# A macaron block on one core: two block-product chunks instead of one in the last down product

## The chip, the core and the metric

The kernel runs on one NeuronCore of a Trainium2 chip. The metric is the device time of one execution in microseconds; the median of the runs counts. Engines go by the profile's names: PE is TensorE (PEld its weight load), DVE VectorE, ACT ScalarE, POOL GpSimd, SP SyncE. SBUF is the memory on the core that all engines work from, PSUM the eight banks into which PE accumulates.

## What is computed

One layer: a feed-forward network at half weight, a mixer of short convolution and gated linear attention, a second feed-forward network at half weight, and a last norm. Sequence 512, model width 1024, hidden width 2816, all in float32. What matters here is the second feed-forward network and the norm behind it:

```python
def rmsnorm(x, g):
    xf = x.astype(jnp.float32)
    y = xf * lax.rsqrt(jnp.mean(xf * xf, axis=-1, keepdims=True) + EPS)
    return (y * g.astype(jnp.float32)).astype(x.dtype)

def swiglu(x, w_gu, w_down):
    g, u = jnp.split(x @ w_gu, 2, axis=-1)
    return (jax.nn.silu(g) * u) @ w_down
...
x = x + FFN_RES_WEIGHT * swiglu(rmsnorm(x, norm_ffn2_g[l]), ffn2_w_gu[l], ffn2_w_down[l])
return rmsnorm(x, final_norm_g)
```

The change is in the last product, `(...) @ w_down` of the second network: 512 x 2816 times 2816 x 1024, that is 22 k tiles of 128.

## The kernel before

**Precision.** Each float32 operand is split into a high half, a cast on ACT, and a low half, a subtraction on DVE; a product is three matmuls (high x high, high x low, low x high).

**Weights.** All weights lie in one array in the order of `PLAN`, in units of 128 x 1024 or less. `STEPS` lists the order in which units are used. The class `Weights` loads units into the pool `f` (10 buffers of 128 x 1024), by DMAs that SP issues, and splits them into `wh` and `wl` (3 buffers each) two units ahead of the one that PE takes (`take`, `issue`). The last four tiles split into `op` instead.

**Block products.** Most of the matrix products are done in the seven-product form of a 2 x 2 block product: seven block products instead of eight, at the price of sums of blocks before and after. The products are called m1, p2, q6, p5, q7, p3, p4. Weight blocks are a11, a12, a21, a22. m1 uses a11, p2 a12, p4 a22. DVE makes s3 = a11 + a21 in another f buffer (line 320), which q7 uses. POOL issues accumulating DMAs (line 310) that add one f buffer to another in place: a22 into a21 (then p5 uses a21), a21 into a11 once m1 is done with it (then q6 uses a11), a11 into a12 once p2 is done with it (then p3 uses a12). The class `Operands` makes the seven operands of the other side; p5, q6, q7 and p4 need a sum on DVE first (lines 556 to 563), made in place, and each is split into two `op` buffers of 128 x 1024 (lines 576 and 577; 14 buffers).

**The last product.** `last_down` works in three stages. First, ten plain k tiles (8 to 17), each 24 matmuls of 512 columns (4 blocks of the sequence, 2 halves of the output, 3 matmuls; lines 778 to 780) into all eight PSUM banks; their operands are split by `split_hid`, two tiles at a time (lines 691 and 692). After them eight adds on DVE carry the banks into the residual `X` (line 787). In between, the operands of the chunk are made, in the order of the list `more`. Then the chunk, k tiles 0 to 7, by seven block products. Each product is taken in two units, which use two weight buffers of 2 k tiles each, and each unit is 12 matmuls of 512 columns into a pair of banks (line 829). After each product two adds of 128 x 512 on DVE carry its pair into `X`. Bank pair b serves m1, q6, q7 and p4, pair a serves p2, pair c serves p5 and p3; six banks are in the pool `ps`, two more in `pa`. Last, four plain tiles (18 to 21, `TAIL`), taken bank by bank, with the last norm and the stores behind each.

**Order.** The order on PE is the order of the code. The queues of the other engines are ordered when the kernel is built: of what is ready and finds a buffer, the instruction that stands first in the code goes first. So loads and splits run ahead as far as their buffers allow. `loads`, `sums` and `pre` in `Weights.phase` say at which step of `STEPS` a chunk's loads, its s3 sums and the tail's loads stand in the code.

Of the kernel before, what the change touches and what calls it, by code (L numbers as in the profile page):

```python
# [15 lines left out]
P = 128  # L16
# [4 lines left out]
KF = DFF // P  # L21
# [19 lines left out]
TAIL = 4  # L41
# [23 lines left out]
def full(mat, kt):  # L65
    return [(mat, k, 1, (0,), 1024) for k in range(kt)]
# [12 lines left out]
HW = 256  # L79
# [24 lines left out]
PLAN = []  # L104
STEPS = []
# [3 lines left out]
def units(us):  # L109
    for u in us:  # L110
        STEPS.append((len(PLAN), None))
        PLAN.append(u)
# [17 lines left out]
CHUNK = 8  # L130
CHUNK_ORDER = ("m1", "p2", "q6", "p5", "q7", "p3", "p4")
CHUNK_STEP = {}


def last_plan(down):
    us = full(down, KF)
    units(us[CHUNK : KF - TAIL])
    firsts = []
    for s in range(2):
        firsts.append(len(PLAN))  # L140
        PLAN.extend((down, 4 * j + 2 * s, 2, (512 * i,), 512) for i in range(2) for j in range(2))
    CHUNK_STEP.update({(s, p): len(STEPS) + 2 * i + s for i, p in enumerate(CHUNK_ORDER)
                       for s in range(2)})
    STEPS.extend((n, p) for p in CHUNK_ORDER for n in firsts)
    units(us[KF - TAIL :])


def ffn_plan(up, down, plain, slow):

    units(group(up, KD, (0, DFF, P, DFF + P), slow))  # L150
    for f in range(2, plain):
        units(single(up, KD, f * P))
        units(single(up, KD, DFF + f * P))
    sets(up, [(s * HW, DFF + s * HW) for s in range(plain // 2, KF // 2)])
    if slow:
        us = full(down, KF)
        units(us[CHUNK : KF - TAIL1])
        sets(down, [(2 * s * HW, (2 * s + 1) * HW) for s in range(D // (2 * HW))])
        units(us[KF - TAIL1 :])
    else:  # L160
        last_plan(down)
    ENDS.append(len(STEPS))
# [33 lines left out]
def block_kernel(ctx: ExitStack, tc: tile.TileContext, xT, vecs, gf, gup, wgl, wts, out):  # L196
    nc = tc.nc
# [12 lines left out]
    def phase(odd, **bufs):  # L210

        stack = ExitStack()
        for n, b in bufs.items():
            pools[n] = stack.enter_context(
                tc.tile_pool(name=n if n != "small" else odd, bufs=b, reuse_waits="tile"))
        return stack

    def tile_of(pool, shape, dtype=F32):
        cnt[0] += 1
        return pools[pool].tile(shape, dtype, tag=pool, name=f"{pool}{cnt[0]}")  # L220
# [4 lines left out]
    def MM():  # L225
        cnt[0] += 1
        return ps.tile([P, S], F32, tag="mm", name=f"mm{cnt[0]}")

    def AUX():
        cnt[0] += 1  # L230
        return pa.tile([P, S], F32, tag="aux", name=f"aux{cnt[0]}")
# [23 lines left out]
    class Weights:  # L255
# [14 lines left out]
        def phase(self, early, first=6):  # L270


            self.early = early
            lo, self.end = self.end, [e for e in ENDS if e > self.end][0]
            for i in range(lo, self.end):
                n, p = STEPS[i]
                if p == "m1" and i in CHUNK_STEP.values():
                    at = CHUNK_STEP[0, "m1"]
                    self.loads.setdefault(at - (4 if i == at else 2), []).append(n)
                    self.sums.setdefault(i, []).append(n)  # L280
                elif p is None and i > lo and STEPS[i - 1][1] is not None and self.end < len(STEPS):
                    self.pre.setdefault(i - 4, []).append(n)
                elif p == "m1":
                    self.loads.setdefault(max(lo, i - first), []).append(n)
                    first = 6
                    self.sums.setdefault(max(lo + 3, i - 3), []).append(n)
            if self.end == len(STEPS):
                c = CHUNK_STEP
                for i, at in enumerate((c[1, "q6"], c[1, "p3"], c[1, "p3"], c[1, "p4"])):
                    self.pre.setdefault(at, []).append(STEPS[self.end - TAIL + i][0])  # L290
            self.fetch(lo)

# [244 lines left out]
    class Operands:  # L537
# [29 lines left out]
        def make(self, p):  # L567
            if p in self.parts:
                return
            i = self.ORDER.index(p)  # L570
            if i > 0:
                self.make(self.ORDER[i - 1])
            v = self.sum(p)
            h, l = (tile_of("op", [P, 1024], F32R) for _ in range(2))
            hv, lv = (t.rearrange("p (k t) -> p k t", t=HW) for t in (h, l))
            nc.scalar.copy(hv, v)  # L576
            nc.vector.tensor_tensor(out=lv, in0=v, in1=hv.bitcast(F32), op=ALU.subtract)  # L577
            self.parts[p] = (h, l)
# [23 lines left out]
    def ffn(up, down, norm, nxt, plain, at):  # L602
# [93 lines left out]
        if nxt is None:  # L696
            return last_down(us, hid, split_hid)
# [67 lines left out]
    def last_down(us, hid, split_hid):  # L765
# [7 lines left out]
        o = [[MM(), MM()] for t in range(NTB - 1)] + [[AUX(), AUX()]]  # L773

        def mm(t, e, k, w, hl):
            wh, wl = (a[:, 512 * e : 512 * (e + 1)] for a in w)
            a, b = (v[:, k % 2, t * P : (t + 1) * P] for v in hl)
            nc.tensor.matmul(o[t][e], a, wh, start=k in (CHUNK, KF - TAIL), stop=False)  # L778
            nc.tensor.matmul(o[t][e], a, wl, start=False, stop=False)  # L779
            nc.tensor.matmul(o[t][e], b, wh, start=False, stop=k in (KF - TAIL - 1, KF - 1))  # L780

        def blocks(t):
            return t.rearrange("p (d i) -> p d i", i=P)
# [1 line left out]
        def add(t, e, bank, by):  # L785
            xt = X[:, 4 * e : 4 * e + 4, t * P : (t + 1) * P]
            nc.vector.scalar_tensor_tensor(out=xt, in0=blocks(bank), scalar=by, in1=xt,
                                           op0=ALU.mult, op1=ALU.add)

        ho = Operands(lambda j, l: hid[:, 4 * j : 4 * j + 4, l * HW : (l + 1) * HW])  # L790
        hls = {k: split_hid(k) for k in (CHUNK, CHUNK + 2)}
        more = [4, 6, 8, "m1", "p2", "p5", "q6", "q7", "p3"]
        for k in range(CHUNK, KF - TAIL):
            w = W.take(us[k])
            for t in range(NTB):
                for e in range(2):
                    mm(t, e, k, w, hls[k - k % 2])
            if more:
                n = more.pop(0)
                if isinstance(n, int):  # L800
                    hls[CHUNK + n] = split_hid(CHUNK + n)
                else:
                    ho.make(n)
        for t in range(NTB):
            for e in range(2):
                add(t, e, o[t][e], 0.5)
        ho.make("p4")


        uses = {"m1": [(0, 0, 0.5)], "p2": [(0, 0, 0.5)], "q6": [(1, 0, 0.5)],  # L810
                "p5": [(1, 1, -0.5)], "q7": [(1, 1, -0.5)], "p3": [(1, 0, 0.5)],
                "p4": [(0, 1, -0.5)]}
        banks = {}
        for p in CHUNK_ORDER:
            b = {"p2": "a", "p5": "c", "p3": "c"}.get(p, "b")
            fresh = b not in banks
            if fresh:
                banks[b] = [MM(), MM()]
            bh, bl = ho.get(p)
            for s in range(2):  # L820
                h, l = W.take()
                for i in range(2):
                    k = 2 * s + i
                    wh, wl = (a[:, 512 * i : 512 * (i + 1)] for a in (h, l))
                    for e in range(2):
                        c = slice(k * HW + e * P, k * HW + (e + 1) * P)
                        to = banks[b][e]
                        for n, (aa, ww) in enumerate(((bh, wh), (bh, wl), (bl, wh))):
                            nc.tensor.matmul(to, aa[:, c], ww,  # L829
                                             start=fresh and k == 0 and n == 0,  # L830
                                             stop=k == 3 and n == 2, skip_group_check=True)
            for l, e, by in uses[p]:
                for t in range(2):
                    add(2 * l + t, e, banks[b][t], by)
        o[:] = [[MM(), MM()] for t in range(NTB - 1)] + [[AUX(), AUX()]]
        w = [W.take(u) for u in us[KF - TAIL :]]
        hl = [split_hid(k) for k in range(KF - TAIL, KF, 2)]
# [41 lines left out]
        with tc.manual_schedule(engines={ENG.PE, ENG.DVE, ENG.Activation}):  # L879
# [4 lines left out]
            for t in range(NTB):  # L884
                sm = front.tile([P, 8], F32, tag="fin", name=f"fin{t}", bufs=2)
                f = [sm[:, i : i + 1] for i in range(6)]
# [502 lines left out]
    with phase("small1", **FFN):  # L1389
        W.phase(1)  # L1390
        n1 = Norm(V_G1)
        for k in range(KD):
            nc.sync.dma_start(x[k], xT[k])
            if k < 2 or k == 3:
                W.issue()
        W.early = 5
        for k in range(KD):
            n1.add(k, sooner=True)
        nm = Norm(V_GM)
        ffn("ffn1_w_gu", "ffn1_w_down", n1, nm, PLAIN1, 5)  # L1400
    with phase("small2", f=10, tp=6, v=4, qk=2, g=1, y=4, small=1):
        W.phase(4, 5)
        n2 = Norm(V_G2)
        mixer(nm, n2)
    with phase("small3", **FFN):
        W.phase(5)
        ffn("ffn2_w_gu", "ffn2_w_down", n2, None, PLAIN2, 5)
# [43 lines left out]
```

## Time and profile before

| | |
|---|---|
| median of 3 runs | 1197.54 us (1197.14 to 1198.35) |
| span of the profiled execution | 1196.1 us |
| its median less its span | 1.4 us |
| PE busy | 1188.1 us, 99% |
| DVE busy | 830.7 us, 69% |
| ACT busy | 587.3 us, 49% |
| ten plain tiles of the last product | 54.42 us, from 1074.95 |
| the chunk | 38.08 us, from 1129.37 |
| the four tail tiles | 21.78 us, from 1167.45 |

The profile gives no time of its own for the profiled execution beside its span; the span runs from the first to the last instruction of the program, and the runs' times contain what lies around it. In the rows of the profile, L829 is line 829 of the kernel before, `out<-in` are the names of the tiles written and read, and what stands in brackets is how long the engine was idle before the instruction and what ended that. `<-` names the releaser, which is inferred. A matmul's duration includes its pipeline, so matmuls overlap, and a stage's length over their count is their pace.

### The profile page before, as it was taken

To read this page: it belongs to the slowest core of one execution; us is meant where nothing else is said; L and a number is where in the kernel's file an instruction comes from. 1 tells how busy PE (TensorE), PEld (TensorE's weight loads), DVE (VectorE), ACT (ScalarE), POOL (GpSimd) and SP (SyncE) were. 2 spreads that over 40 slices of the span, in tenths; PEclk is the share of its full clock that TensorE was granted. 3 is DMA by queue.
4 is the path that set the end of the run, shared out by engine and by line. 5 is a ranking of instruction groups with operands and counts; after the bars stand their busy time and mean duration, and the time that the engine had idled before them with its cause. 6 is when DMAs were issued, how large, how long until landed. Compare 5 with 4: busy or idle time off the path is not lost.

```text
span 1196.1 us, 19145 instructions
## 1 busy us (share of the span) xinstructions
PE 1188.1 (99%) x7858; PEld 1095.6 (92%) x7858; DVE 830.7 (69%) x997; ACT 587.3 (49%) x730; POOL 101.2 (8%) x137
## 2 busy tenths in 40 slices
PE   9999999999999999999999999999999999999997
PEld 8899999988988889999999998888889999998886
DVE  7976566844787765858678686555597656675685
ACT  6564444622354465646454574324355455562353
POOL 0011111000110001011011100100001111100100
PEclk9999999999999999999999999999999999999999
DMA  9377777533473225767767766613338777763431
GB/s 346 87 207 187 180 184 187 176 101 80 104 270 106 88 66 146 201 183 188 191 179 175 190 185 211 203 48 141 120 74 209 167 188 173 186 180 108 93 95 70
DMA packets 57607, 187.65 MB, mean 157 GB/s; under 512 B 6480, under 2 KB 10704, under 8 KB 57520
## 3 DMA queue, kind: packets, MB, share of 16 engines
q1 hardware_dynamic: 36912, 124.27, 29.5%
q0 software_dynamic: 15968, 57.68, 26.1%
q10 hardware_dynamic: 4640, 4.49, 1.2%
q8 instruction: 61, 1.00, 0.3%
q14 instruction: 26, 0.21, 0.1%
HBM read 124.55 MB, written 8.39 MB: 111 GB/s over the span
## 4 chain that ended last, share of the span: by engine, by line
PE 99%; ACT 0%; DVE 0%; issue 0%; POOL 0%; POOLq 0%
PE mm L528 54%; PE mm L387 7%; PE mm L363 6%; PE mm L365 6%; PE mm L364 6%; PE mm L829 3%; PE mm L779 2%; PE mm L780 2%; PE mm L778 2%; PE mm L405 1%; PE mm L406 1%; PE mm L404 1%; PE aux L1120 1%; PE aux L363 1%; PE aux L364 1%; PE aux L780 1%
## 5 line engine op out<-in xcount | busy, mean ns | idle before, releaser
L528 PE MATMUL mm<-op,wh 128*128 128x256 f32 x3584 | 648.0, 283 | 0.0
L335 ACT CAST wh<-f 128x1024 fp32r<-128x1024 f32 (+1 forms) x319 | 333.4, 1046 | 467.3 <-PE mm L528 235.3
L528 PEld LDWEIGHTS mm<-op,wh 128*128 128x128 f32 x3584 | 558.9, 192 | 1.0
L336 DVE TENSOR_TENSOR wl<-f,wh 128x1024 fp32r<-128x1024 f32 (+1 forms) x319 | 387.6, 1218 | 203.8 <-ACT wh L335 199.0
L528 PE MATMUL mm<-op,wl 128*128 128x256 f32 x1792 | 507.3, 283 | 0.0
L528 PEld LDWEIGHTS mm<-op,wl 128*128 128x128 f32 x1792 | 343.3, 192 | 0.3 <-DVE wl L336 0.2
L310 POOL DMA_DIRECT2D f<-f x102 | 88.2, 864 | 932.8 <-DVE wl L336 481.0
L363 PE MATMUL mm<-op,wh 128*128 128x512 f32 x340 | 132.7, 390 | 0.0
L365 PE MATMUL mm<-op,wl 128*128 128x512 f32 x340 | 132.5, 390 | 0.0
L364 PE MATMUL mm<-op,wh 128*128 128x512 f32 x340 | 132.3, 389 | 0.0
L365 PEld LDWEIGHTS mm<-op,wl 128*128 128x128 f32 x340 | 63.8, 188 | 13.4
L364 PEld LDWEIGHTS mm<-op,wh 128*128 128x128 f32 x340 | 63.8, 188 | 13.1
L363 PEld LDWEIGHTS mm<-op,wh 128*128 128x128 f32 x340 | 63.8, 188 | 13.1
L387 PE MATMUL mm<-op,wh 128*128 128x512 f32 x256 | 64.2, 393 | 0.0
L387 PEld LDWEIGHTS mm<-op,wh 128*128 128x128 f32 x256 | 48.5, 190 | 10.3
L533 ACT COPY tp<-mm 128x512 f32<-128x512 f32 x90 | 52.3, 581 | 0.0
L576 ACT CAST op<-hid 128x1024 fp32r<-128x1024 f32 x28 | 29.4, 1050 | 37.4 <-PE aux L779 20.7
L577 DVE TENSOR_TENSOR op<-hid,op 128x1024 fp32r<-128x1024 f32 x28 | 34.2, 1221 | 18.5 <-ACT op L576 18.5
L320 DVE TENSOR_TENSOR f<-f,f 128x1024 f32<-128x1024 f32 x34 | 41.6, 1223 | 0.9
L829 PE MATMUL mm<-wh,op 128*128 128x512 f32 x112 | 34.6, 389 | 0.0
L387 PE MATMUL mm<-op,wl 128*128 128x512 f32 x128 | 34.2, 389 | 0.0
L387 PEld LDWEIGHTS mm<-op,wl 128*128 128x128 f32 x128 | 24.0, 188 | 5.0
(253 smaller groups left out, 1136.6 us busy)
## 6 DMA issues: line engine op xcount, KB each, us to landing
f<-wts SPq DMA_DIRECT2D x219, 512.0 KB, 4.1
f<-f POOLq DMA_DIRECT2D x102, 512.0 KB, 4.8
X<-xT SPq DMA_DIRECT2D x8, 256.0 KB, 5.2
xs<-X POOLq DMA_DIRECT2D x8, 256.0 KB, 6.3
ga<-tp ACTq DMA_DIRECT2D x8, 256.0 KB, 4.0
gb<-tp ACTq DMA_DIRECT2D x8, 256.0 KB, 4.9
tp<-ga SPq DMA_DIRECT2D x8, 256.0 KB, 6.1
tp<-gb SPq DMA_DIRECT2D x8, 256.0 KB, 2.8
```

The source lines that it names most:

```text
L310: nc.gpsimd.dma_start(out_, a, accum_op=ALU.add)
L320: nc.vector.tensor_tensor(out=s3, in0=a11, in1=a21, op=ALU.add)
L335: nc.scalar.copy(h[:, :w], raw[:, :w])
L336: nc.vector.tensor_tensor(out=l[:, :w], in0=raw[:, :w], in1=h[:, :w].bitcast(F32), op=ALU.subtract)
L363: nc.tensor.matmul(o, wh, ah, start=first, stop=False)
L364: nc.tensor.matmul(o, wh, al, start=False, stop=False)
L365: nc.tensor.matmul(o, wl, ah, start=False, stop=last)
L387: nc.tensor.matmul(o[c], w[:, s : s + P], a[k], start=k == 0 and j == 0, stop=k == kt - 1 and j == 2)
L528: nc.tensor.matmul(to, ww[:, s], aa[:, t], start=fresh and k == 0 and e == 0 and j == 0, stop=k == 3 and j == 2, skip_group_check=True)
L533: nc.scalar.copy(v, o)
L780: nc.tensor.matmul(o[t][e], b, wh, start=False, stop=k in (KF - TAIL - 1, KF - 1))
L829: nc.tensor.matmul(to, aa[:, c], ww, start=fresh and k == 0 and n == 0, stop=k == 3 and n == 2, skip_group_check=True)
```

## The change

Instead of one chunk of eight k tiles, two chunks are used (k tiles 2 to 9 and 10 to 17), and two plain tiles (0 and 1) stand ahead instead of ten. The four tail tiles stay. The chunks are chained: the second chunk's m1 comes between the first's p3 and p4, its p2 behind p4. The order within a chunk is the same otherwise. Operands are made one product at a time, four ahead. The second chunk's loads are put 8 and 4 steps ahead of its m1, its two sums at its m1. Each chunk has bank pairs of its own out of the same pools. No buffer is added.

```diff
+FILL = 2
+CHUNKS = 2
+
+def chunk_order():
+    seq = [(0, "m1"), (0, "p2")]
+    for c in range(CHUNKS):
+        seq += [(c, p) for p in ("q6", "p5", "q7", "p3")]
+        seq += [(c + 1, "m1"), (c, "p4"), (c + 1, "p2")] if c + 1 < CHUNKS else [(c, "p4")]
+    return seq
...
 def last_plan(down):
     us = full(down, KF)
-    units(us[CHUNK : KF - TAIL])
+    units(us[:FILL])
...
+    for c, p in chunk_order():
+        for s in range(2):
+            CHUNK_STEP[c, s, p] = len(STEPS)
+            STEPS.append((firsts[c, s], p))
     units(us[KF - TAIL :])
...
                 if p == "m1" and i in CHUNK_STEP.values():
-                    at = CHUNK_STEP[0, "m1"]
-                    self.loads.setdefault(at - (4 if i == at else 2), []).append(n)
+                    c, s = next(k[:2] for k, at in CHUNK_STEP.items() if at == i)
+                    at = CHUNK_STEP[c, 0, "m1"] - ((4, 2), (8, 4))[c][s]
+                    self.loads.setdefault(max(lo, at), []).append(n)
                     self.sums.setdefault(i, []).append(n)
...
-        ho = Operands(lambda j, l: hid[:, 4 * j : 4 * j + 4, l * HW : (l + 1) * HW])
-        hls = {k: split_hid(k) for k in (CHUNK, CHUNK + 2)}
-        more = [4, 6, 8, "m1", "p2", "p5", "q6", "q7", "p3"]
-        for k in range(CHUNK, KF - TAIL):
+        def operands(c):
+            f = FILL + CHUNK * c
+            return Operands(lambda j, l: hid[:, f + 4 * j : f + 4 * j + 4, l * HW : (l + 1) * HW])
...
+        def make(n):
+            for c, p in makes[:n]:
+                ho[c].make(p)
+            del makes[:n]
+
+        hl = split_hid(0)
+        make(2)
+        for k in range(FILL):
             w = W.take(us[k])
             for t in range(NTB):
                 for e in range(2):
-                    mm(t, e, k, w, hls[k - k % 2])
...
+                    mm(t, e, k, w, hl)
+            make(1)
...
         banks = {}
-        for p in CHUNK_ORDER:
-            b = {"p2": "a", "p5": "c", "p3": "c"}.get(p, "b")
+        for c, p in seq:
+            b = c, {"p2": "a", "p5": "c", "p3": "c"}.get(p, "b")
             fresh = b not in banks
             if fresh:
                 banks[b] = [MM(), MM()]
-            bh, bl = ho.get(p)
+            make(1)
+            bh, bl = ho[c].get(p)
```

More of the change, by code (lines that the diff above doesn't have):

```diff
@@ L132 @@
 CHUNK_STEP = {}
+FILL = 2
[6 more added lines that the diff above has]
+    return seq
 def last_plan(down):
     us = full(down, KF)
-    units(us[CHUNK : KF - TAIL])
[L138 to L144, printed above, removed]
+    units(us[:FILL])
+    firsts = {}
+    for c in range(CHUNKS):
+        for s in range(2):
+            firsts[c, s] = len(PLAN)
+            PLAN.extend((down, FILL + CHUNK * c + 4 * j + 2 * s, 2, (512 * i,), 512)
+                        for i in range(2) for j in range(2))
+    for c, p in chunk_order():
+        for s in range(2):
+            CHUNK_STEP[c, s, p] = len(STEPS)
+            STEPS.append((firsts[c, s], p))
     units(us[KF - TAIL :])
@@ L288, in phase @@
                 c = CHUNK_STEP
-                for i, at in enumerate((c[1, "q6"], c[1, "p3"], c[1, "p3"], c[1, "p4"])):
+                for i, p in enumerate(("q6", "p3", "p3", "p4")):
+                    at = c[CHUNKS - 1, 1, p]
                     self.pre.setdefault(at, []).append(STEPS[self.end - TAIL + i][0])
@@ L777, in mm @@
             a, b = (v[:, k % 2, t * P : (t + 1) * P] for v in hl)
-            nc.tensor.matmul(o[t][e], a, wh, start=k in (CHUNK, KF - TAIL), stop=False)
+            nc.tensor.matmul(o[t][e], a, wh, start=k in (0, KF - TAIL), stop=False)
             nc.tensor.matmul(o[t][e], a, wl, start=False, stop=False)
-            nc.tensor.matmul(o[t][e], b, wh, start=False, stop=k in (KF - TAIL - 1, KF - 1))
+            nc.tensor.matmul(o[t][e], b, wh, start=False, stop=k in (FILL - 1, KF - 1))
         def blocks(t):
@@ L788, in add @@
                                            op0=ALU.mult, op1=ALU.add)
-        ho = Operands(lambda j, l: hid[:, 4 * j : 4 * j + 4, l * HW : (l + 1) * HW])
-        hls = {k: split_hid(k) for k in (CHUNK, CHUNK + 2)}
-        more = [4, 6, 8, "m1", "p2", "p5", "q6", "q7", "p3"]
-        for k in range(CHUNK, KF - TAIL):
+        def operands(c):
+            f = FILL + CHUNK * c
+            return Operands(lambda j, l: hid[:, f + 4 * j : f + 4 * j + 4, l * HW : (l + 1) * HW])
+        ho = [operands(c) for c in range(CHUNKS)]
+        seq = chunk_order()
+        makes = [(c, p) for c in range(CHUNKS) for p in Operands.ORDER]
+        def make(n):
[5 more added lines that the diff above has]
+        for k in range(FILL):
             w = W.take(us[k])
@@ L796, in last_down @@
                 for e in range(2):
-                    mm(t, e, k, w, hls[k - k % 2])
[L798 to L803, printed above, removed]
+                    mm(t, e, k, w, hl)
+            make(1)
         for t in range(NTB):
@@ L806, in last_down @@
                 add(t, e, o[t][e], 0.5)
-        ho.make("p4")
         uses = {"m1": [(0, 0, 0.5)], "p2": [(0, 0, 0.5)], "q6": [(1, 0, 0.5)],
@@ L825, in last_down @@
                     for e in range(2):
-                        c = slice(k * HW + e * P, k * HW + (e + 1) * P)
+                        at = slice(k * HW + e * P, k * HW + (e + 1) * P)
                         to = banks[b][e]
                         for n, (aa, ww) in enumerate(((bh, wh), (bh, wl), (bl, wh))):
-                            nc.tensor.matmul(to, aa[:, c], ww,
+                            nc.tensor.matmul(to, aa[:, at], ww,
                                              start=fresh and k == 0 and n == 0,
```

## Prediction

> **What bounds the kernel now.** I read the page first, then the busy time of three stages, then the end of the chain that ended last.
>
> ```profile
> span 1196.1 us, 19145 instructions
> ...
> PE 1188.1 (99%) x7858; PEld 1095.6 (92%) x7858; DVE 830.7 (69%) x997; ACT 587.3 (49%) x730; POOL 101.2 (8%) x137
> ...
> PEclk9999999999999999999999999999999999999999
> ```
>
> TensorE is busy for the whole span at full granted clock. VectorE has 31% idle on average, but an average over stages says little about the one stage that the change touches. So that stage comes next. The boundaries are the first plain k tile of the second down product, the first product of the chunk, the first matmul of the four tail tiles, and the last matmul.
>
> ```profile
> 1074.95:1129.37 54.42, 54.42 (x241) 45.04 (x241) 30.66 (x30) 15.96 (x17) 3.45 (x4) 1.00 0.38 103
> 1129.37:1167.45 38.08, 38.08 (x170) 31.53 (x169) 31.40 (x35) 20.92 (x22) 1.72 (x2) 1.00 0.35 91
> 1167.45:1189.23 21.78, 21.76 (x97) 17.68 (x95) 14.51 (x38) 7.80 (x20) 0.00 (x0) 1.00 0.13 49
> ```
>
> The columns after the length are busy time on PE, weight load, DVE, ACT and POOL, then granted clock, DMA share and GB/s. PE has no hole in any of the three. In the chunk stage DVE is already busy for 31.40 of 38.08 us. The chain that ended last says the same of PE:
>
> ```profile
> 1129.37 38.08 PE mm L829 x168
> ...
> 1188.99 0.24 PE aux L780
> 1189.25 0.70 DVE X L848
> ```
>
> The chunk's 168 matmuls are one unbroken piece: 38.08 / 168 = 0.2267 us each. The ten plain tiles give the same pace: 54.42 / 240 = 0.2268. I use this pace and not the 389 ns of a single matmul in the groups, because those overlap. The profiled span of 1196.1 us is 1.4 us below the median of the runs, 1197.54; I work inside the span and leave that 1.4 us as it is.
>
> **What goes away.** Eight plain k tiles have 8 x 24 = 192 matmuls. A chunk has 7 products x 2 units x 12 = 168. All are 512 wide. So PE loses 24 matmuls: 24 x 0.2267 = 5.44 us, all on the path that sets the end, as PE has no idle time to lose instead. The tail and the stages before do not change. With no new wait the result is 1197.54 - 5.44 = 1192.1 us. Everything else below asks how much of this is given back. New places in time: the two plain tiles end at 1074.95 + 48 x 0.2267 = 1085.84, which I call T0, and the two chunks then last 76.16 us. I number the units of 12 matmuls from T0; each lasts 2.72 us, so unit i starts at T0 + 2.72 i.
>
> **What is added on ACT, POOL and SP.** ACT gets 14 weight casts and 7 operand casts for the 8 + 4 that go: 9 more, about 1 us each, on an engine busy for 20.92 of 38.08 us. SP has the same eight 512 KB loads. POOL has six more accumulating DMAs. I take no loss of throughput there, since DMA share in these stages is 0.13 to 0.38. What counts for them is latency, below.
>
> **What is added on DVE.** A chunk has 14 low halves of weights, 2 weight sums, 7 low halves of operands and 4 operand sums, 27 instructions of 1024 columns, and 14 adds of 512 columns. Their durations:
>
> ```profile
> L336 DVE TENSOR_TENSOR wl<-f,wh 128x1024 fp32r<-128x1024 f32 x12 | 14.5, 1219 | 3.0 <-ACT wh L335 3.0
> L787 DVE SCALAR_TENSOR_TENSOR X<-mm,X 128x512 f32<-128x512 f32 x14 | 9.0, 681 | 2.7 <-PE mm L829 2.7
> ...
> L577 DVE TENSOR_TENSOR op<-hid,op 128x1024 fp32r<-128x1024 f32 x6 | 7.3, 1222 | 14.4 <-ACT op L576 14.4
> L320 DVE TENSOR_TENSOR f<-f,f 128x1024 f32<-128x1024 f32 x2 | 2.4, 1224 | 0.1
> L558 DVE SCALAR_TENSOR_TENSOR hid<-hid 128x1024 f32<-128x1024 f32 x1 | 1.2, 1217 | 0.0
> ```
>
> At these durations a chunk costs 27 x 1.22 + 14 x 0.68 = 42.5 us, more than its 38.08 us of PE. But back to back, instructions of DVE overlap a little. The DVE timeline of a stretch in which it never rested:
>
> ```profile
> 1147.00 1.21 DVE L336 TENSOR_TENSOR op<-f,op 128x1024 fp32r<-128x1024 f32 x1
> 1148.13 1.22 DVE L336 TENSOR_TENSOR wl<-f,wh 128x1024 fp32r<-128x1024 f32 x1
> 1149.27 1.22 DVE L336 TENSOR_TENSOR op<-f,op 128x1024 fp32r<-128x1024 f32 x1
> 1150.41 1.22 DVE L336 TENSOR_TENSOR wl<-f,wh 128x1024 fp32r<-128x1024 f32 x1
> 1151.54 1.28 DVE L787 SCALAR_TENSOR_TENSOR X<-mm,X 128x512 f32<-128x512 f32 x2
> 1152.74 1.21 DVE L336 TENSOR_TENSOR op<-f,op 128x1024 fp32r<-128x1024 f32 x1
> ```
>
> From start to start a long one takes 1.135 us and two adds take 1.20. That is the price when DVE is the scarce engine, and I take it: 27 x 1.135 + 14 x 0.60 = 39.0 us for a chunk. From the plain tiles to the end of the second chunk there are 54 long ones of the chunks, 3 of the plain tiles (two weights, one operand) and 6 that prepare the tail, 63 in all, and 28 + 8 adds. Some are done by T0. The kernel before makes seven operand pairs by 1078, as fast as the finished sets free their buffers; after the change these seven are the plain pair and six of the first chunk. With them go that chunk's four operand sums, its two weight sums and four weights (two plain, the first product's two): 17. Six of the 17 are sums; before, only two sums stand ahead of 1085.84, so four are new there. Is there room?
>
> ```profile
> 1060.00:1081.90 21.90, 21.90 (x157) 20.67 (x156) 19.44 (x21) 15.19 (x17) 0.86 (x1) 1.00 0.63 192
> 1081.90:1085.84 3.94, 3.94 (x19) 3.28 (x18) 1.10 (x1) 0.18 (x1) 0.00 (x0) 1.00 0.37 131
> ```
>
> DVE is free for 2.46 + 2.84 = 5.3 us; four sums take 4.5 to 4.9. They just fit. So 46 long ones and 36 adds are left: 52.2 + 21.6 = 73.8 us in 76.16 us, 97% of DVE. I expect no loss of PE from this alone, but no reserve either.
>
> [...]
>
> **Where I expect the wait.** The weights of the second chunk live in the ten f buffers. A chunk fills all ten: eight blocks and two sums. The second chunk's loads follow the first's releases one by one. That a load starts when a buffer comes free, the kernel before shows: the low half of 1141.38 is the last reader of its block, and the next load starts right behind it.
>
> ```profile
> 1141.38 1.23 DVE L336 TENSOR_TENSOR wl<-f,wh 128x1024 fp32r<-128x1024 f32 x1 [0.30 <-ACT wh L335]
> ...
> 1142.63 0.33 SPq L306 DMA_DIRECT2D f<-wts  x1
> ```
>
> The eight loads take the first eight releases (q6, p5, q7 and p3 of both halves), the last of them about T0 + 27, early enough. The two sum buffers of the second chunk take what is left: the a22 blocks, which p4 reads last. And p4 (units 14, 15) stands after the second chunk's m1. Behind the sum hang an accumulate of a22 into a21, another of a21 into a11, and only then the weights of q6 (units 18, 19). Prices of the links:
>
> ```profile
> 1132.13 1.06 ACT L335 CAST wh<-f 128x1024 fp32r<-128x1024 f32 x1 [0.94 <-PE mm L829]
> 1133.22 1.22 DVE L336 TENSOR_TENSOR wl<-f,wh 128x1024 fp32r<-128x1024 f32 x1 [0.29 <-ACT wh L335]
> ...
> 1110.90 1.22 DVE L320 TENSOR_TENSOR f<-f,f 128x1024 f32<-128x1024 f32 x1
> 1112.66 0.86 POOL L310 DMA_DIRECT2D f<-f  x1 [48.69 <-DVE f L320]
> 1115.44 1.23 DVE L320 TENSOR_TENSOR f<-f,f 128x1024 f32<-128x1024 f32 x1
> 1118.48 0.86 POOL L310 DMA_DIRECT2D f<-f  x1 [4.96 <-issue]
> ...
> DMA to landing us min/median/max: 4.5/4.6/6.0
> ```
>
> A cast starts when the buffer of three units before is free; cast and low half take 2.31 us. Sum to issue takes 0.54 beyond the sum's 1.22 (1.8 in the other row). A landing takes 4.6 us, 6.0 beside another transfer (the last line: the accumulates from 1040 us on).
> Unit 14: cast at T0 + 32.64, ready 34.95, sum 36.2, issue 36.7, landed 41.3, issue 41.5, landed 46.1, weights of unit 18 ready at 48.4. PE wants them at 48.96: in time, by half a microsecond.
> Unit 15: ready 37.67, sum 38.9, issue 39.4, landed 45.4 (it lies beside the other pair, so 6.0), issue 45.6, landed 50.2 to 51.6, weights of unit 19 ready at 52.5 to 53.9. PE wants them at 51.68: 0.8 to 2.2 us late. I take 1.5, the middle.
>
> Behind the waiting cast stand, on ACT, operand and tail casts; behind the waiting low half, on DVE, adds and operand halves that are wanted a product later. They are late by the same 1.5 us as PE and cost nothing more, as long as DVE is not behind already. Later products find their weights: p3 hangs on one more accumulate, landed about T0 + 56, and is wanted at T0 + 65. PSUM's six banks suffice, since p2's pair is free when the second m1 starts. Sum: -5.44 + 1.5 = -3.9 us, 1193.6 us, a span of about 1192.2.
>
> **Rivals.** What a measurement of this kernel can tell from no change is about 0.2%, 2.4 us. The forecast case is faster by more, so it holds for waits up to 3.0 us.
>
> First rival: the chain is longer. With both landings at 6.0 and POOL's 1.8 us, unit 19 is ready at 37.67 + 1.22 + 1.8 + 6.0 + 0.2 + 6.0 + 2.31 = 55.2, 3.5 us late. Then the clock may come in:
>
> ```profile
> 1190.00:1191.00 1.00, 0.00 (x0) 0.00 (x0) 0.83 (x2) 0.97 (x3) 0.00 (x0) 1.00 0.59 223
> 1191.00:1192.00 1.00, 0.00 (x0) 0.00 (x0) 0.80 (x5) 0.13 (x2) 0.00 (x0) 0.61 0.00 0
> ```
>
> About 2 us after the last matmul the granted clock falls towards half. At half clock PE does half its work, so each microsecond of it costs 0.5. With 1 to 4 us of it the wait costs 4.0 to 5.5: 1196.1 to 1197.6 us, within 0.2%. That the sums of both halves and all tail loads stay out of each other's way speaks against it. [...]
>
> Second rival: DVE sets the pace at 1.22 and 0.68 us. Then the 46 and 36 cost 56.1 + 24.5 = 80.6 us, 4.5 over, and the time is 1197.54 - 5.44 + 4.5 = 1196.6, again within 0.2%. The gap-free stretch above speaks against it; that each low half waits for a cast somewhere speaks for it.
>
> Third rival, on the other side: DVE as the bound, and the six sums of the first chunk not made ahead because the DVE before T0 is full. That adds up to 6 x 1.22 = 7.3: 88 us of DVE work in 76.16, 11.8 late, 1203.9 us. It is slower than before by over 0.2% from a lateness of 7.8 on, which is from the third late sum on. For it: 19.44 of 21.90 us are taken there. Against it: the four new sums fit, and an early lateness has many products in which to shrink.
>
> That the change doesn't save its 24 matmuls is not likely: they are counted in the code.
>
> **How the numbers follow.** Forecast 0.57; longer chain 0.13; DVE at full durations 0.11; sums late 0.19. Faster 0.57, within 0.2% 0.24, slower 0.19. The range begins at 1191.9, where nothing waits, and takes in both middle rivals and the lower part of the third, up to 1199.5; the forecast's own range is 1192.1 to 1195.1.
>
> **What would show it.** Right: two chunk stages with 336 matmuls; PE without a hole until the second chunk's q6, there one of 1 to 2 us that ends with the low half of a weight, after an accumulate; DVE busy over 90% through both chunks. Wrong: holes of PE in the first chunk, or before every product (DVE is the bound); no hole at q6 (the sums got their buffers sooner); a granted clock under 1.00 before the tail.

## The result and the profile after

The change makes the kernel slower by 0.2%: 1200.41 us (median of 16 runs, 1199.51 to 1201.56) against 1197.96 us (16 runs of the kernel before beside them, 1197.14 to 1198.67). The ratio is 1.0022, with a 95% interval of 1.0016 to 1.0029. The forecast was 1193.6, and the time lies above its range.

The page of the changed kernel hardly gives the reason away:

```profile
span 1199.1 us, 19159 instructions
...
PE 1186.8 (99%) x7834; PEld 1092.3 (91%) x7834; DVE 855.1 (71%) x1026; ACT 596.4 (50%) x739; POOL 106.1 (9%) x143
...
PEclk9999999999999999999999999999999999999989
```

The 24 matmuls are gone, 7834 for 7858. TensorE (PE) is still busy 99% of the span. Only a single 8 in the row of the granted clock is new. A slice there is 30 us long, so what it hides has to be looked for in shorter windows. Those of the last product (length; busy time of PE, weight load, DVE, ACT, POOL; clock; DMA share; GB/s):

```profile
1085.90:1130.00 44.10, 43.89 (x193) 35.78 (x192) 43.74 (x50) 24.58 (x24) 4.03 (x5) 1.00 0.61 155
1130.00:1139.00 9.00, 6.30 (x27) 4.53 (x25) 4.51 (x5) 0.82 (x1) 2.40 (x4) 0.99 0.93 175
1139.00:1146.00 7.00, 6.26 (x15) 4.62 (x16) 5.92 (x6) 2.58 (x4) 1.32 (x2) 0.53 0.90 170
1146.00:1170.00 24.00, 24.00 (x107) 19.87 (x106) 21.42 (x23) 15.47 (x17) 0.00 (x0) 1.00 0.24 83
...
1139.00:1140.00 1.00, 0.72 (x1) 0.29 (x1) 0.74 (x1) 0.22 (x1) 0.46 (x1) 0.50 0.09 16
...
1146.00:1147.00 1.00, 1.00 (x6) 0.82 (x5) 0.28 (x1) 1.00 (x2) 0.00 (x0) 1.00 0.91 373
```

Up to 1130 and from 1146 on PE has no idle time worth the name. Between them lie two losses in a row: 2.7 us of idle time ahead of 1139, then 7 us at a clock of 0.53. In that second stretch PE counts as busy for 6.26 us, yet it does 15 matmuls where 7 us at the pace of full clock, 0.2267 us each, would hold 31. So the busy share tells of the hole and is silent on the clock. Windows of 1 and 2 us around the edges put the half clock from about 1138.8 to 1145.6, 6.8 us.

What PE waits for stands in its timeline:

```profile
1136.04 0.39 PE L854 MATMUL mm<-wh,op 128*128 128x512 f32 x1
1139.28 0.80 PE L854 MATMUL mm<-wh,op 128*128 128x512 f32 x1 [2.85 <-ACT wh L353]
1140.53 0.80 PE L854 MATMUL mm<-wl,op 128*128 128x512 f32 x1 [0.46 <-DVE wl L354]
```

This is the first unit of the second chunk's q6 (unit 18 in the prediction's count); a matmul takes 0.80 us there in place of 0.39. The table of waits (total, times, longest) has the cast on ACT for which PE waits:

```profile
ACT wh L353 <- DMA f<-f: 9.7, 2, 8.3
```

It waited 8.3 us for an accumulate. The chain that ended last, followed back from there:

```profile
1121.82 1.22 DVE wl L354
1123.04 0.07 DVE hid L579
1123.11 0.98 issue
1124.09 1.23 DVE f L338
1125.32 0.03 POOLq L328
1125.35 0.47 issue
1125.82 0.01 POOLq L328
1125.84 12.24 DMA f<-f x3
...
1138.18 1.05 ACT wh L353
1139.26 1.24 DVE wl L354
1140.49 0.04 issue
1140.53 29.64 PE mm L854 x119
```

Line 338 is the second chunk's first s3 sum. The low half ahead of it, of 1121.82, is the last reader of the a22 block whose buffer the sum takes. Behind the sum come the accumulates, 12.24 us of them, then cast, low half and PE.

From the starts of PE's matmuls, first plain one to last of the tail, the last product takes 116.39 us; before, it took 114.04. The difference of 2.35 is nearly the whole of the 2.45 between the medians. With the 5.44 that the 24 matmuls were worth, 7.8 us are given back: 6.9 in units 16 to 18 (0.46, 3.02 and 3.40 over the 2.72 of a unit), 0.6 in units 0 and 2, 0.2 ahead of the first chunk, 0.1 in unit 19.

### The profile page after: what moved, and what is told of

It is laid out like the page before. It is cut to its first block, busy times and chain, and to the rows that moved or that the text cites. A ratio compares the mean times of both kernels' runs of the same rounds, so it can differ in the third digit from the quotient of the medians.

```text
span 1199.1 us, 19159 instructions
## 1 busy us (share of the span) xinstructions
PE 1186.8 (99%) x7834; PEld 1092.3 (91%) x7834; DVE 855.1 (71%) x1026; ACT 596.4 (50%) x739; POOL 106.1 (9%) x143
## 5 line engine op out<-in xcount | busy, mean ns | idle before, releaser
L353 ACT CAST wh<-f 128x1024 fp32r<-128x1024 f32 (+1 forms) x325 | 339.7, 1046 | 482.2 <-PE mm L546 237.2
L354 DVE TENSOR_TENSOR wl<-f,wh 128x1024 fp32r<-128x1024 f32 (+1 forms) x325 | 394.8, 1218 | 200.2 <-ACT wh L353 195.3
L546 PEld LDWEIGHTS mm<-op,wl 128*128 128x128 f32 x1792 | 343.3, 192 | 0.5 <-DVE wl L354 0.4
L328 POOL DMA_DIRECT2D f<-f x108 | 93.2, 866 | 934.1 <-DVE wl L354 492.9
L383 PE MATMUL mm<-op,wl 128*128 128x512 f32 x340 | 132.5, 390 | 0.0
L383 PEld LDWEIGHTS mm<-op,wl 128*128 128x128 f32 x340 | 63.8, 188 | 13.3
L854 PE MATMUL mm<-wh,op 128*128 128x512 f32 x224 | 71.5, 400 | 2.9 <-ACT wh L353 2.9
L854 PEld LDWEIGHTS mm<-wh,op 128*128 128x128 f32 x224 | 43.3, 193 | 12.7 <-ACT wh L353 3.3
L594 ACT CAST op<-hid 128x1024 fp32r<-128x1024 f32 x35 | 36.7, 1049 | 21.2 <-PE mm L382 8.8
L595 DVE TENSOR_TENSOR op<-hid,op 128x1024 fp32r<-128x1024 f32 x35 | 42.7, 1220 | 4.3 <-ACT op L594 4.3
L854 PE MATMUL mm<-wl,op 128*128 128x512 f32 x112 | 44.9, 401 | 0.8 <-DVE wl L354 0.6
```

Of the source, the lines that this page charges most:

```text
L328: nc.gpsimd.dma_start(out_, a, accum_op=ALU.add)
L353: nc.scalar.copy(h[:, :w], raw[:, :w])
L354: nc.vector.tensor_tensor(out=l[:, :w], in0=raw[:, :w], in1=h[:, :w].bitcast(F32), op=ALU.subtract)
L383: nc.tensor.matmul(o, wl, ah, start=False, stop=last)
L546: nc.tensor.matmul(to, ww[:, s], aa[:, t], start=fresh and k == 0 and e == 0 and j == 0, stop=k == 3 and j == 2, skip_group_check=True)
L854: nc.tensor.matmul(to, aa[:, at], ww, start=fresh and k == 0 and n == 0, stop=k == 3 and n == 2, skip_group_check=True)
```

## The experiments

My theory after this: the sums get their buffers too late, the late chain makes a hole, and the hole brings the half clock. Rivals: DVE, full through both chunks, is the bound; or the accumulates disturb one another. The kernel before was timed beside each series: its median is 1197.65 us beside the experiments e1 to e4 and 1197.82 beside the others.

**Sums in buffers of their own** (`e1_sums_elsewhere`). The first four k tiles of the hidden activations are dead by then, so no memory is added:

```diff
+            self.spare = {}
...
-                self.raw[n].append(tile_of("f", [P, 1024]))
+                self.raw[n].append(self.spare[n] if n in self.spare else tile_of("f", [P, 1024]))
...
+        for s in range(2):
+            n = STEPS[CHUNK_STEP[1, s, "m1"]][0]
+            W.spare[n] = hid[:, 2 * s : 2 * s + 2].rearrange("p k t -> p (k t)")
```

> The second chunk's two s3 sums go into hidden tiles 0 to 3, which nothing reads any more by then, and not into f buffers. So they need not wait for p4 to release a22; nothing else changes. Theory A (the buffers: sum after p4, two accumulates, then q6 late, then half clock): the sums run once the loads have landed, up to 10 us sooner; no hole of PE before the second chunk's q6, no half clock, and of the 8.0 us given back only the small waits (0.4 to 1.1 us, DVE late by under half a microsecond at three units and in the up stage) stay: 1192.5 to 1193.5 us. Theory B (DVE is the bound in both chunks, 43.74 of 44.10 us busy): the time lost at q6 turns up elsewhere, before other products; 1196 us or more.

Measured: 1193.26 us, ratio 0.9964 (0.9951 to 0.9977). The DVE timeline has the two sums:

```profile
1115.30 1.22 DVE L339 TENSOR_TENSOR hid<-f,f 128x1024 f32<-128x1024 f32 x1
...
1117.57 1.22 DVE L339 TENSOR_TENSOR hid<-f,f 128x1024 f32<-128x1024 f32 x1
```

The window of the two chunks:

```profile
1085.45:1161.99 76.54, 76.35 (x335) 62.90 (x336) 74.86 (x82) 42.45 (x43) 7.74 (x9) 1.00 0.61 151
```

And the landings of the accumulates' line from 1120 to 1140:

```profile
DMA to landing us min/median/max: 4.9/6.4/8.1
```

The sums run some 8 us sooner, counted from the first product; PE is busy for 76.35 of 76.54 us at full clock, and the last product takes 109.40 us. DVE is busy for 74.86 of those 76.54 us, 98%. So even a DVE as full as this hardly holds PE up here; that rival falls. And landings of up to 8.1 us harm nothing here, where the chain starts in time. A second series (`e9_best_again`):

> The kernel of e1 (second chunk's sums in hidden tiles), timed in five rounds for a narrower interval: 1193.0 to 1193.6 us, a ratio of 0.9960 to 0.9970 to the kernel before.

It gave 1194.08 us (1193.54 to 1194.85), 0.9969 (0.9956 to 0.9981): the time is a little above what was expected, the ratio within it. This version beats both kernels.

**p4 ahead of the next m1** (`e2_p4_first`). The a22 blocks are then read two units sooner:

```diff
-        seq += [(c + 1, "m1"), (c, "p4"), (c + 1, "p2")] if c + 1 < CHUNKS else [(c, "p4")]
+        seq += [(c, "p4"), (c + 1, "m1"), (c + 1, "p2")] if c + 1 < CHUNKS else [(c, "p4")]
```

> The first chunk's p4 is put ahead of the second chunk's m1, so that p4 lets go of a22 two units (5.44 us) sooner against the second q6; the sums stay in f buffers. Theory A: the chain from sum to q6 starts 5.4 us sooner and the hole was 2.9 us, so no hole and no half clock: 1192.5 to 1193.5 us. Theory B: 1196 us or more. If the hole closes only in part (theory C: the four accumulates slow one another whenever they start), a wait of 0.5 to 1 us stays and the clock stays up: 1194 us.

Measured: 1197.33 us, 0.9998 (0.9989 to 1.0007), in theory B's range: more than half of the gain expected by theory A stayed out. The timelines of DVE and PE:

```profile
1122.33 1.22 DVE L338 TENSOR_TENSOR f<-f,f 128x1024 f32<-128x1024 f32 x1
...
1136.54 1.22 DVE L595 TENSOR_TENSOR op<-hid,op 128x1024 fp32r<-128x1024 f32 x1 [2.64 <-ACT op L594]
...
1138.95 0.50 PE L854 MATMUL mm<-wl,op 128*128 128x512 f32 x1 [2.02 <-DVE wl L354]
```

Two windows behind the hole:

```profile
1138.00:1140.00 2.00, 1.05 (x5) 0.87 (x6) 2.00 (x3) 1.65 (x2) 0.86 (x1) 1.00 1.00 186
1140.00:1142.00 2.00, 2.00 (x6) 1.62 (x5) 2.00 (x4) 0.00 (x0) 0.00 (x0) 0.50 1.04 199
```

The sum came only 2.3 us sooner, counted from the first product. The low half of q6 then stood behind an operand half on DVE, which itself waited 2.64 us for its cast, and PE had a hole of 2.02 us; one more microsecond later the clock fell to half, for about 3.4 us. To see whether the buffers or the order make this hole, both edits together (`e7_elsewhere_p4_first`):

> Sums in hidden tiles as in e1, and p4 ahead of the second m1 as in e2. If buffers and order are two ways to the same end, nothing more is won: 1193 to 1194 us, no hole at q6. If e2's rest (a hole of 2.0 us behind a DVE that had an operand's half queued ahead of q6's weight) comes from the order and not from the late chain, it shows again: 1196 to 1197 us.

Measured: 1197.43 us, 0.9997 (0.9988 to 1.0006), with the same hole of 2.02 us and half clock behind it as in p4 first, and a time within 0.1 us of it. With p4 first the first sum stands at 1122.14 though its buffer is free and all eight loads had landed by 1118.34, since DVE takes what is ready in the order of the code. Here it is the order, as the second branch has it, at 0.4 us above its time.

**Less work on DVE** (`e4_no_adds_first_chunk`).

```diff
-            for l, e, by in uses[p]:
+            for l, e, by in uses[p] if c else ():
```

> Leaves out the 14 adds of the first chunk's products into the residual (so the residual lacks them): 8.4 us of DVE work less, nothing else. The buffers and the accumulates stay as they are. If DVE's queue (theory B) made the sum late, the sums start at once behind p4's low halves, 2 us sooner than 1124.09, the hole shrinks to about 1 us, and the clock stays at 1.00: 1194 to 1195 us. If the buffers alone set it (theory A without DVE's part), the hole stays 2.5 to 3 us with the half clock behind it: 1199 to 1200 us.

Measured: 1198.70 us, 1.0007 (0.9998 to 1.0017), between the two. The sum stood at 1122.90, some 1.2 us sooner than in the changed kernel when counted from the first product; the holes were 2.47 and 0.76 us, and the half clock held for one stretch of 3.4 us. Taking 8.4 us of work from DVE thus gains some 1.7 us, about as much as the intervals can tell apart; in the traces the last product is 1.4 us shorter (114.95 us). DVE's load sets a part of the lateness, not the pace.

**PE kept busy in the hole** (`e3_pe_kept_busy`), by 13 matmuls that nobody reads:

```diff
+            if (c, p) == (1, "p2"):
+                idle = AUX()
+                for i in range(13):
+                    nc.tensor.matmul(idle, bh[:, :P], bh[:, :512], start=True, stop=True)
```

> Thirteen idle matmuls (512 columns, on an operand of p2, into a bank that nothing reads) are added on PE before the second chunk's q6; nine of them stand right ahead of it. They take no wait away; they only keep PE busy for about 2.0 of the 2.9 us of the hole. If the half clock follows from the hole, granted clock stays 1.00 and the two units behind it take 2.7 to 3.3 us instead of 6.12 and 2.85: about 3 us won, 1197 to 1198 us. If the 6.12 us of that unit were late weights and not the clock, nothing is won or the matmuls cost up to 1 us: 1200 to 1201 us.

Measured: 1201.82 us, 1.0034 (1.0022 to 1.0046): the clock came out as expected, the time did not. Up to the last matmul the clock is 1.00, and unit 18 takes 3.91 us in place of 6.12, yet units 20 and 21 now take 4.03 and 4.08. ACT's timeline shows why:

```profile
1147.34 1.05 ACT L353 CAST op<-f 128x1024 fp32r<-128x1024 f32 x1 [2.10 <-DMA f<-wts]
1148.29 1.04 ACT L353 CAST wh<-f 128x1024 fp32r<-128x1024 f32 x1
```

A cast for the tail waits 2.10 us for its load, and the cast for the chunk stands behind it in the queue. In the changed kernel, held up by the half clock, that cast waited only 0.37 us, and PE had no hole there. Three of the tail's loads in dead tiles of `hid` as well (`e5_busy_tail_elsewhere`, `spare` as in the first experiment):

> The thirteen idle matmuls of e3, and beside them three of the tail's four weight loads go into hidden tiles 4 to 9 (dead by then), so that they land early. In e3 the clock stayed up, but PE then waited 1.15 + 0.94 us at 1149 to 1151, behind ACT, which stood 2.1 us at a tail cast whose load had just landed. If that cast is the next wait, it goes: no hole at units 20 and 21, stage shorter by 2.5 to 3.0 us than in e3, 1198.5 to 1199.5 us. If the wait comes from elsewhere (DVE full after the hole), it stays and the time stays at 1201 to 1202 us.

Measured: 1199.43 us, 1.0015 (1.0005 to 1.0024), with 0.36 us left of those holes. So the second wait is what the tail's loads had made. Idle matmuls don't pay here: 13 x 0.2267 = 2.9 us of PE go for them, and the late chain stays late.

**One chain of accumulates instead of two** (`e6_one_chain`).

```diff
-                self.add(a21, a22)
+                if n != STEPS[CHUNK_STEP[1, 1, "m1"]][0]:
+                    self.add(a21, a22)
```

and in the same way for the two other accumulates of the second chunk's second half.

> Leaves out the three accumulating DMAs of the second chunk's second half (so that half's q6, p5 and p3 use plain blocks); the first half's chain, the buffers and all else stay as in the changed kernel. Theory A with theory C (the four accumulates slow one another: landings of 7.2 and 6.1 us instead of 4.5): the first half's chain lands in 4.5 + 4.5 us, 2.6 us sooner than 1138.08, the hole at the second q6 falls from 2.85 to under 0.7 us, the clock stays up: 1193.5 to 1194.5 us. If transfers do not matter and only the sum's start does, the first half's chain is as late as before: hole 2.5 us or more, half clock, 1199 us or more.

Measured: 1199.64 us, 1.0018 (1.0008 to 1.0027), with a hole of 2.38 us: the gain expected by theories A and C together stayed out. The time lies in the range of the other branch, though the hole is just under its 2.5 us. The second accumulate of the chain was issued 1.3 us after the first had landed, at 1130.84, as POOL's timeline shows:

```profile
1132.16 0.86 POOL L328 DMA_DIRECT2D f<-f  x1 [5.00 <-issue]
```

It took 5.87 us although no other accumulate ran. Beside it the view of the DMA queues (packets, MB, share) has one fetch of instructions from 1132 to 1139:

```profile
q8 instruction: 1, 0.02, 1.3%
```

So the other half's accumulates are not what makes the chain long, or not alone.

**The sums on POOL** (`e8_sums_on_pool`), on top of the first experiment:

```diff
-                nc.vector.tensor_tensor(out=s3, in0=a11, in1=a21, op=ALU.add)
+                chunk = n >= STEPS[CHUNK_STEP[0, 0, "m1"]][0]
+                (nc.gpsimd if chunk else nc.vector).tensor_tensor(out=s3, in0=a11, in1=a21,
+                                                                  op=ALU.add)
```

> e1 with the four s3 sums of the two chunks on POOL instead of DVE: 4.5 us less on DVE, of which 2.3 before the first chunk. In e1 PE still loses 0.13 and 0.49 us at the first two products, to a low half that DVE makes late. If DVE's load there is the cause, these go: 1192.5 to 1193 us. If POOL is slow at the sum (over 4 us) or holds up its own DMA issues, the first chunk's q6 gets late: 1194 us or more.

Measured: 1199.57 us, 1.001 (1.000 to 1.002), spread from 1196.28 to 1201.68, in the range of the second branch: the gain stayed out. One of POOL's sums and what DVE did beside it:

```profile
1120.76 3.21 POOL L340 TENSOR_TENSOR hid<-f,f 128x1024 f32<-128x1024 f32 x1 [5.85 <-DMA f<-wts]
...
1121.62 3.43 DVE L357 TENSOR_TENSOR wl<-f,wh 128x1024 fp32r<-128x1024 f32 x1
```

A low half that takes 1.22 us on DVE elsewhere took 3.43 beside it. In this way four instructions of DVE took 6.9 us longer in all, more than the 4.5 us that the four sums take on DVE. Two of the four lie ahead of the first chunk, and behind them PE has a hole of 2.24 us before its first product:

```profile
1089.09 0.47 PE L860 MATMUL mm<-wh,op 128*128 128x512 f32 x1 [2.24 <-DVE X L808]
```

The clock stays at 1.00 behind this hole, in the windows that the last section shows.

**A hole by itself** (`e10_hole_alone`): the best version, with PE made to wait ahead of q6 for a small DMA.

```diff
+            if (c, p) == (1, "p2"):
+                z = front.tile([P, 24], F32, tag="zero", name="zero")
+                side = AUX()
+                nc.sync.dma_start(z, fill)
+                nc.tensor.matmul(side[:24, :24], z, h[:, :24].bitcast(F32), start=True, stop=True)
+                nc.sync.dma_start(z, fill)
+                for t in banks[1, "b"]:
+                    nc.tensor.matmul(t[:24, :24], z, z, start=False, stop=False,
+                                     skip_group_check=True)
```

> e1, and a hole of PE made on purpose at the same place, before the second chunk's q6: a DMA of 24 zero columns may start only when a small matmul at the end of p2 has read its target, and two small matmuls that add zeros to q6's banks wait for it. No weight and no operand is late here, so the price of a hole stands alone. The hole will be 1.9 to 2.5 us by the small stores' landing in the tail (2.0 us). If a hole of 2 us brings the half clock, as in e2 and in the changed kernel, the units behind it run at half for one window of 3.4 us or two, and the time rises by the hole and 1.7 us or 3.4 us more: 1197 to 1199 us. If the half clock needs a longer hole, it rises by the hole alone: 1195.2 to 1195.8 us.

Measured: 1200.48 us, 1.0021 (1.0012 to 1.0030), 6.4 us over the 1194.08 of the same kernel without the hole, and above the expected range. The timeline of PE has the second hole:

```profile
1140.69 0.28 PE L868 MATMUL mm<-zero 128*24 128x24 f32 x4 [2.22 <-DMA zero<-fill]
```

Two windows behind it:

```profile
1142.00:1143.00 1.00, 1.00 (x4) 0.78 (x3) 1.00 (x1) 0.00 (x0) 0.00 (x0) 0.54 0.86 319
1143.00:1144.00 1.00, 1.00 (x4) 0.74 (x3) 0.06 (x1) 0.00 (x0) 0.00 (x0) 0.50 0.34 135
```

There were two holes, 1.14 and 2.22 us, as the edit delays a cast too, which waits for the added small matmul. Together 3.4, and 3.4 us of half clock at 0.5 make another 1.7: 5.1 of the 5.9 by which the last product grew. The hole and the clock behind it are enough to turn the best version into one as slow as the changed kernel.

## Why the prediction was wrong

**The saving was right.** 24 matmuls, 5.44 us, all on the path: with the sums in other buffers the last product fell from 114.04 to 109.40 us, 4.64 less, and the remaining 0.8 is lost around the first chunk's first products. Most of it (0.5) is in unit 2, where a matmul waits for a low half that DVE makes late, behind the eight adds of the plain tiles; the prediction had no term for it.

**The place and the mechanism were right.** PE is without a real hole up to the second chunk's q6, and the chain is the predicted one: p4's release, sum, two accumulates, cast, low half. That the mechanism costs the time is shown by the first experiment, which removes only the buffers' part of it.

**The step that failed is the chain of unit 14**, summed up to weights ready at T0 + 48.4, half a microsecond ahead of PE. With T0 now 1086.24, each link measured:

| unit 14, us after T0 | predicted | measured |
|---|---|---|
| low half of a22 ready | 34.95 | 36.8 |
| sum done | 36.2 | 39.1 |
| first accumulate landed | 41.3 | 44.1 |
| second issued | 41.5 | 44.65 |
| second landed | 46.1 | 51.84 |
| weights of q6 ready | 48.4 | 54.2 |

Two terms carry nearly all of the 5.8 us. One is the wait in the queues ahead of the sum, 2.9 us, which the working put at nothing: it took 97% of DVE as harmless and then let the cast, the low half and the sum run the moment their inputs were there. The timelines of ACT and DVE in the changed kernel show what stood in the way:

```profile
1119.72 1.06 ACT L353 CAST wh<-f 128x1024 fp32r<-128x1024 f32 x1 [0.20 <-PE mm L854]
...
1120.69 1.22 DVE L595 TENSOR_TENSOR op<-hid,op 128x1024 fp32r<-128x1024 f32 x1
1121.82 1.22 DVE L354 TENSOR_TENSOR wl<-f,wh 128x1024 fp32r<-128x1024 f32 x1
1122.95 1.22 DVE L579 TENSOR_TENSOR hid<-hid 128x1024 f32<-128x1024 f32 x1
1124.09 1.22 DVE L338 TENSOR_TENSOR f<-f,f 128x1024 f32<-128x1024 f32 x1
```

The cast that this low half needs ended at 1120.78, 0.8 us later than forecast, as PE had by then lost 0.6 us in units 0 and 2. Then an operand half held DVE, and an operand sum went ahead of the s3 sum, about one instruction each. Not all of this is DVE's load. With the 14 adds left out (less work on DVE), the low half is ready at T0 + 36.7 as before, because its cast then stands behind an operand's cast on ACT, for which ACT sits idle 1.44 us until PE is done; only the sum is sooner, at 37.9. So 1.2 of the 2.9 us are shown to come with DVE's load; the rest is what PE lost before and what else stands ahead in the queues. The prediction had written "as long as DVE is not behind already" into its own argument, and applied it only to what comes after. The other term is the second landing, 4.6 us in the forecast and 7.2 in the trace, in a queue in which the other half's accumulate had started 1.5 us ahead of it. POOL's timeline:

```profile
1129.41 0.86 POOL L328 DMA_DIRECT2D f<-f  x1 [2.72 <-ACT wh L353]
1130.89 0.86 POOL L328 DMA_DIRECT2D f<-f  x1 [0.62 <-issue]
```

And the landings of the two:

```profile
DMA to landing us min/median/max: 4.5/5.9/7.2
```

The prediction gave that neighbour to unit 15 alone, with 6.0 us; by the same price unit 14's weights would have been ready at 49.8, 0.8 us late. So unit 18 was late, not unit 19 by 1.5 us, and PE stood still for 2.85 + 0.46 us.

**The clock was left out of the forecast.** The prediction had it in its first rival, at 1 to 4 us. It held for 6.8 us, in 5.9 of which PE worked; at 0.5 each that is some 2.9 us, nearly half of the 6.4 lost in units 17 and 18. So the first rival was right in kind and still too cheap: 4.0 to 5.5 us there, 6.4 in the trace. Its 1 to 4 us of half clock were an estimate of mine that no trace of the kernel before shows; the runs showed stretches of 3.4 us (p4 first, less work on DVE, a hole by itself) and of 6.8 us (the changed kernel). Nor does a hole's length alone tell whether half clock follows: it followed a single hole of 2.02 us in the second experiment, and did not follow one of 2.24 us with the sums on POOL. The last section has them side by side.

**The other rivals fell.** DVE at full durations, or late by its sums, would have held PE up throughout. With DVE busy for 98% the first experiment has no such wait beyond the 0.8 us named above. And the six sums of the first chunk were made ahead in the changed kernel, the last of them at 1083.23, 3 us before T0.

**Open.** How the 7.2 us of the second landing divide between the neighbouring accumulate and a fetch of instructions (0.02 MB between 1130 and 1138) was not settled: the run with one chain still had a landing of 5.87. Nor was the time that POOL let pass ahead of an issue, 0.62 and 2.73 us in the changed kernel and 5.00 with one chain, for which the profile names no releaser.

## What to carry to other kernels

When one stage is chained to the next in the same buffers, list which release each new tile takes, and if a long chain starts at the last release, look for dead tiles elsewhere before anything else: here that is worth 6 to 7 us and costs no memory. For each link of such a chain, look for what stands ahead of it in the queue of its engine, and add about one instruction's wait, even if the engine's throughput suffices. And take into account that a hole of PE can cost more than its length: here the half clock behind holes of 2.02 and of 2.85 + 0.46 us cost some 1.7 and 2.9 us on top, while a hole of 2.24 us had none behind it.

## What the runs showed of the hardware that I had not expected

- **Short holes were followed by half clock, and not by their length alone.** Single holes of 2.02 us (p4 first) and 2.85 us (the changed kernel) were followed by 3.4 and 6.8 us of it; one of 2.24 us (sums on POOL) was not, nor were holes of 1.15 and 0.94 us (PE kept busy). Here are a stretch with the hole and the one behind it of p4 first, and then two that hold the hole of the sums on POOL:

```profile
1136.58:1139.99 3.41, 1.39 (x7) 0.86 (x6) 3.41 (x4) 2.00 (x2) 0.86 (x1) 1.00 0.99 189
1139.99:1143.40 3.41, 3.41 (x10) 2.64 (x9) 3.41 (x5) 0.59 (x1) 0.00 (x0) 0.50 0.98 201
...
1085.24:1088.65 3.41, 1.61 (x8) 0.99 (x6) 3.41 (x4) 3.41 (x4) 0.01 (x1) 1.00 1.03 192
1088.65:1092.07 3.42, 2.98 (x13) 2.50 (x14) 3.42 (x7) 0.14 (x1) 0.85 (x1) 1.00 0.82 156
```

In p4 first the half clock began at 1139.99, 1.04 us after PE had resumed at 1138.95; in the changed kernel it began at about 1138.8, before PE resumed at 1139.28. What decides whether and for how long it comes was not shown: no run moved a hole in time to test it.

- **The sums on POOL held DVE up.** A sum of 128 x 1024 in float32 took 2.4 to 5.4 us on POOL, and one instruction of DVE beside each of the four took 2.2 to 3.4 us in place of 1.22.
- **A landing is no constant.** The same 512 KB accumulate took from 4.5 us (the changed kernel) to 8.1 us (sums in buffers of their own). The longest was in a stretch with accumulates issued 2.5 to 4.8 us apart; but 5.87 us were also seen with no other accumulate in flight (one chain).
